# Both feed-forward down products with tokens stationary: 16 of 22 k tiles in two seven-product sets, sums added from PSUM, the first product's result turned back by transposes

## The chip, the cores and the metric

The kernel runs on one core of a Trainium2 chip. The metric is the device time of one launch in microseconds. Of the kernel before there are three timed runs and one profiled run.

## What is computed

One block of a language model, in float32, for 512 tokens of width 1024: a feed-forward part with half weight, a mixer (a gated convolution and gated linear attention, merged by sigmoid gates), a second feed-forward part with half weight, and a last norm.

```python
def swiglu(x, w_gu, w_down):
    g, u = jnp.split(x @ w_gu, 2, axis=-1)
    return (jax.nn.silu(g) * u) @ w_down          # w_gu 1024 x 5632, w_down 2816 x 1024

merged = jax.nn.sigmoid(ga) * y_conv + jax.nn.sigmoid(gb) * y_gla

for l in range(DEPTH):                            # DEPTH = 1
    x = x + 0.5 * swiglu(rmsnorm(x, norm_ffn1_g[l]), ffn1_w_gu[l], ffn1_w_down[l])
    x = x + hybrid_mixer(rmsnorm(x, norm_mix_g[l]), w_in[l], ...)
    x = x + 0.5 * swiglu(rmsnorm(x, norm_ffn2_g[l]), ffn2_w_gu[l], ffn2_w_down[l])
return rmsnorm(x, final_norm_g)
```

The change concerns the two products with `w_down` (22 tiles of 128 along k, 1024 outputs), what lies between the first one and the mixer, and the places at which the mixer loads the gates `gb`.

## The kernel before, in words

**Precision.** Every operand is split into a high part (a cast) and a low part (the rest), and every product is three matmuls: high x high, high x low, low x high. For weights the cast is made by ACT (L310) and the subtraction by DVE (L311); for activations the same pair stands at L550 and L551, in a norm at L416 and L417.

**Layout.** `x` is kept transposed, as eight tiles X of 128 features x 512 tokens. In most products the weights are stationary and 512 or 256 columns of tokens move. At the end X must have tokens in rows; so during the second feed-forward part's up product its blocks are turned by four PE transposes each (`natural`, L713), and the second down product has the tokens stationary and 512 columns of weights moving.

**Sets.** Where a matrix is taken as 2 x 2 blocks, a *set* computes its four block products as seven products (named m1, p2, q6, p5, q7, p4, p3) of sums and differences of blocks. That needs sums of weights (one by DVE, L297, and the rest by DMAs that accumulate, issued on POOL, L288), sums of activations (DVE, L530 to L537) and additions of the results, which share three pairs of PSUM banks: a (p2), b (m1, q6, q7, p4), c (p5, p3). A *wide set* is the form for the second down product: 8 k tiles, 512 tokens, 1024 outputs. Two of them take k tiles 0 to 15; each product has two units of four moving blocks, a step of the plan each. The last six k tiles are done plainly.

**Order of the work.** The weights' order is a hand-made list: `STEPS` has an entry for each unit that is cast, `PLAN` for each block that is loaded (L92 to L150). `W.take()` casts two steps ahead of use. The loads of a set are issued six steps ahead of its first product. Plain units are prefetched `early` steps ahead (L271 to L277; 5 in the feed-forward parts, 4 in the mixer), but the look ahead stops at the first step that belongs to a set. The order of the instructions on each engine is then made by the framework's scheduler from the order of the program and its waits.

**The first down product** (L682 to L705) is plain: weights stationary, 22 k tiles x 8 output tiles, eight PSUM banks. For each output tile in turn the last two k tiles are done, DVE adds half of the bank into X (L703), and `nxt.add` (L404 to L426) makes the norm's parts for the mixer: high part by ACT, low part by DVE, square by ACT, and its sum by DVE.

**The second down product** (`last_down`, L716 on) runs the wide sets in the order `SEQ` (L127): m1, p2, q6, p5, q7, p4, p3. ACT copies m1, q6 and q7 out of PSUM, scaled (L756); DVE adds a bank to such a copy (L759, L764, L773); POOL adds the sum to X (L761, L766, L775); p4 is added by DVE from PSUM into X (L769).

**The mixer** begins with q, k and the low-rank gate (`gate_k`, L934), which take the normed tiles in turn. POOL's queue saves all eight X tiles to DRAM (`xs`, L873). The gates ga and gb are computed, saved to DRAM (L1263 for gb) and read back by `gate` (a load on SP's queue at L1307 or L1309, a sigmoid on ACT, L1311). The eight tiles of gb are read within the two sets of `w_out_gla`, at their products m1, p5 and p4 (`gla_done`, L1340 on). The squares of the attention's output are cast at L389 and summed by PE at L1104.

## Time and profile before

| | |
|---|---|
| three timed runs, us | 1211.93, 1209.31, 1205.89; median 1209.31 |
| profiled run, us | 1207.32, its span 1205.6 |
| granted clock of TensorE, mean | 0.996 |
| first down product, first to last matmul | 231.18 to 350.89 us of the span |
| second down product's two wide sets | 1079.75 to 1165.93 us |
| POOL's instructions | 155, of them 108 accumulating DMAs |

How to read it: PE is TensorE's matmuls, PEld its weight loads, which overlap them; DVE is VectorE, ACT ScalarE, POOL GpSimd, SP the engine on whose queue the loads are issued. A row of the timeline has start, duration, engine, line, operation, output<-inputs and shape; in brackets stands how long the engine was idle ahead of it and what ended that. A row of a group has the count, then the total of busy time in us and the mean of one in ns, then the idle time ahead. A row of waits has the total in us, the number and the longest. A row of windows has the busy time of each engine, the granted clock, the share of DMA and GB/s.

### The profile page before, as it was taken

Reading aid. Unit: us, or ns where it says so; the run is one execution under the profiler, and the core shown is the slowest. Engines: PE = TensorE matmul, PEld = TensorE weight load, DVE = VectorE, ACT = ScalarE, POOL = GpSimd, SP = SyncE. Lnnn points to the kernel's source line nnn. Section 1 sums busy time; section 2 is a strip of 40 time slices with the busy share of each in tenths; the row PEclk is TensorE's granted clock in tenths of the full one; section 3 lists DMA queues with packets and bytes.
Section 4 is the critical chain, followed back from the end, with each engine's and each line's share of the span. In section 5 each row is a group of like instructions: output and inputs, shape, how many; then the busy total and the mean of one; then the engine's idle time right before and its main releaser. Section 6 shows DMA issues by size and latency. Waiting matters only on the chain.

```text
span 1205.6 us, 19145 instructions
## 1 busy us (share of the span) xinstructions
PE 1187.8 (99%) x7834; PEld 1092.1 (91%) x7834; DVE 840.7 (70%) x990; ACT 612.1 (51%) x762; POOL 130.0 (11%) x155
## 2 busy tenths in 40 slices
PE   9999999999999999999999999999999999999987
PEld 8899999988888889999999998898889999997776
DVE  7976666732277765868688687586597656589865
ACT  6555455532254465646554575454355455466453
POOL 0011111000010001101011100200001111113420
PEclk9999999999999999999999999999999999999999
DMA  9477777531162325767777756752447777757711
GB/s 349 95 200 189 178 187 186 167 105 53 52 241 92 88 70 150 213 171 186 194 184 176 192 182 183 208 149 93 161 99 194 189 175 177 183 143 197 161 50 70
DMA packets 59496, 190.81 MB, mean 158 GB/s; under 512 B 6576, under 2 KB 12848, under 8 KB 59408
## 3 DMA queue, kind: packets, MB, share of 16 engines
q1 hardware_dynamic: 37936, 124.27, 29.6%
q0 software_dynamic: 16832, 60.83, 27.3%
q10 hardware_dynamic: 4640, 4.49, 1.2%
q8 instruction: 61, 1.00, 0.3%
q14 instruction: 27, 0.22, 0.1%
HBM read 124.55 MB, written 8.39 MB: 110 GB/s over the span
## 4 chain that ended last, share of the span: by engine, by line
PE 89%; DVE 4%; DMA 3%; issue 2%; ACT 1%; POOL 0%; SPq 0%; DVEq 0%; ACTq 0%; POOLq 0%
PE mm L502 50%; PE mm L362 7%; PE mm L340 6%; PE mm L338 6%; PE mm L339 6%; DVE wl L311 2%; DMA f<-f 1%; PE mm L380 1%; PE mm L381 1%; PE mm L379 1%; DMA g<-gb 1%; DMA f<-wts 1%; PE aux L340 1%; PE aux L338 1%; PE aux L339 1%
## 5 line engine op out<-in xcount | busy, mean ns | idle before, releaser
L502 PE MATMUL mm<-op,wh 128*128 128x256 f32 x3584 | 649.9, 284 | 3.3 <-ACT tp L507 3.3
L310 ACT CAST wh<-f 128x1024 fp32r<-128x1024 f32 (+1 forms) x325 | 339.6, 1046 | 483.6 <-PE mm L502 225.2
L311 DVE TENSOR_TENSOR wl<-f,wh 128x1024 fp32r<-128x1024 f32 (+1 forms) x325 | 400.4, 1235 | 242.0 <-ACT wh L310 230.2
L502 PEld LDWEIGHTS mm<-op,wh 128*128 128x128 f32 x3584 | 560.2, 192 | 4.9 <-ACT tp L507 3.9
L502 PE MATMUL mm<-op,wl 128*128 128x256 f32 x1792 | 507.9, 284 | 0.0
L502 PEld LDWEIGHTS mm<-op,wl 128*128 128x128 f32 x1792 | 344.0, 192 | 0.1
L288 POOL DMA_DIRECT2D f<-f x108 | 93.3, 869 | 847.0 <-DVE wl L311 470.1
L340 PE MATMUL mm<-op,wl 128*128 128x512 f32 x324 | 126.4, 390 | 0.1
L338 PE MATMUL mm<-op,wh 128*128 128x512 f32 x324 | 126.5, 390 | 0.0
L339 PE MATMUL mm<-op,wh 128*128 128x512 f32 x324 | 126.1, 389 | 0.0
L340 PEld LDWEIGHTS mm<-op,wl 128*128 128x128 f32 x324 | 60.8, 188 | 13.2 <-DVE wl L311 0.5
L339 PEld LDWEIGHTS mm<-op,wh 128*128 128x128 f32 x324 | 60.8, 188 | 12.6
L338 PEld LDWEIGHTS mm<-op,wh 128*128 128x128 f32 x324 | 60.8, 188 | 12.4
L362 PE MATMUL mm<-op,wh 128*128 128x512 f32 x256 | 63.5, 390 | 0.3 <-DVE op L413 0.3
L362 PEld LDWEIGHTS mm<-op,wh 128*128 128x128 f32 x256 | 47.9, 188 | 10.6 <-ACT acc L422 0.4
L507 ACT COPY tp<-mm 128x512 f32<-128x512 f32 x96 | 55.8, 581 | 1.2 <-DVE tp L1238 1.0
L747 PE MATMUL mm<-wh,op 128*128 128x512 f32 x112 | 44.4, 398 | 4.1 <-ACT wh L310 2.4
L749 PE MATMUL mm<-wl,op 128*128 128x512 f32 x112 | 45.0, 401 | 2.1 <-DVE wl L311 2.0
L297 DVE TENSOR_TENSOR f<-f,f 128x1024 f32<-128x1024 f32 x36 | 44.0, 1221 | 1.8 <-DMA f<-f 1.0
L751 PE MATMUL mm<-wh,op 128*128 128x512 f32 x112 | 44.2, 395 | 0.0
L551 DVE TENSOR_TENSOR op<-hidw,op 128x1024 fp32r<-128x1024 f32 x28 | 36.0, 1297 | 1.3 <-ACT op L550 1.3
L550 ACT CAST op<-hidw 128x1024 fp32r<-128x1024 f32 x28 | 29.1, 1047 | 11.0 <-DVE hidw L597 4.0
(270 smaller groups left out, 1157.6 us busy)
## 6 DMA issues: line engine op xcount, KB each, us to landing
f<-wts SPq DMA_DIRECT2D x219, 512.0 KB, 4.3
f<-f POOLq DMA_DIRECT2D x108, 512.0 KB, 5.0
X<-xT SPq DMA_DIRECT2D x8, 256.0 KB, 4.9
xs<-X POOLq DMA_DIRECT2D x8, 256.0 KB, 5.4
ga<-tp ACTq DMA_DIRECT2D x8, 256.0 KB, 3.9
gb<-tp ACTq DMA_DIRECT2D x8, 256.0 KB, 4.1
g<-gb SPq DMA_DIRECT2D x8, 256.0 KB, 3.8
tp<-ga SPq DMA_DIRECT2D x8, 256.0 KB, 4.8
```

The source lines that it names most:

```text
L288: nc.gpsimd.dma_start(out_, a, accum_op=ALU.add)
L310: nc.scalar.copy(h[:, :w], raw[:, :w])
L311: nc.vector.tensor_tensor(out=l[:, :w], in0=raw[:, :w], in1=h[:, :w].bitcast(F32), op=ALU.subtract)
L338: nc.tensor.matmul(o, wh, ah, start=first, stop=False)
L339: nc.tensor.matmul(o, wh, al, start=False, stop=False)
L340: nc.tensor.matmul(o, wl, ah, start=False, stop=last)
L362: nc.tensor.matmul(o[c], w[:, s : s + P], a[k], start=k == 0 and j == 0, stop=k == kt - 1 and j == 2)
L502: nc.tensor.matmul(to, ww[:, s], aa[:, t], start=fresh and k == 0 and e == 0 and j == 0, stop=k == 3 and j == 2, skip_group_check=True)
L507: nc.scalar.copy(v, o)
L747: nc.tensor.matmul(o[t], bh[:, s], wh, start=fresh and k == 0, stop=False, skip_group_check=True)
L749: nc.tensor.matmul(o[t], bh[:, s], wl, start=False, stop=False, skip_group_check=True)
L751: nc.tensor.matmul(o[t], bl[:, s], wh, start=False, stop=k == 3, skip_group_check=True)
```

## The change

Four things are done.

1. The first down product takes the second one's form, and both are now one function, `down_product`: k tiles 0 to 15 as two wide sets, tokens stationary, then six plain k tiles. In the first, the results are kept in eight tiles `S_` (four token blocks x two halves of the outputs): the first result that comes to a tile is copied there by ACT, the others are added by DVE. The last four k tiles are done half by half; after each block of the second half, `back(i)` turns one 128-feature tile of the sum back by four transposes, DVE adds half of it into X, and `nxt.add(i)` follows. That does tiles 0 to 3; tiles 4 to 7 are done in `gate_k` of the mixer's k steps 0 to 3 (`norm.late`), and their save to DRAM with them.
2. The additions change in both. The order of the products is m1, p5, q6, p2, q7, p3, p4; no bank of the pair b is used by two products that follow each other. Pair a is kept over both sets and the plain k tiles: m1 of the first set is copied into it by ACT, and both sets' p2 and the plain tiles accumulate on it (the plain ones also on c, where the second set's p3 stays). Everything else DVE adds from PSUM, in the second product directly into X. POOL's twelve additions are gone. A class `DownOperands` makes the sums of activations, one of them already during the up product.
3. `Weights.fetch` looks past steps of sets, as long as the step being issued is one of a set. Two of the first product's last four weight units are put in the pool `op`, as the second product's are.
4. The eight tiles of gb are read and passed through the sigmoid during the eight steps of `w_out_conv` (`early_gate`), ahead of the sets of `w_out_gla`, into tiles that are free then.

```diff
-SEQ = ("m1", "p2", "q6", "p5", "q7", "p4", "p3")
+SEQ = ("m1", "p5", "q6", "p2", "q7", "p3", "p4")
...
-    if not slow:
-        wide_sets(down)
-    units(full(down, KF)[0 if slow else 8 * WIDE :])
+    wide_sets(down)
+    units(full(down, KF)[8 * WIDE :])
...
                 if p is None and n not in self.raw:
                     self.raw[n] = self.dma(n)
-                elif p is not None:
+                elif p is not None and STEPS[at][1] is None:
                     break
...
-            late = at >= len(STEPS) - TAIL
+            late = at >= len(STEPS) - TAIL or ENDS[0] - TAIL <= at < ENDS[0] - 2
...
+        def add(c, l, t, bank, scale):
+            at = 2 * l + t, c
+            if nxt is not None and at not in S_:
+                S_[at] = T()
+                nc.scalar.activation(S_[at], bank, AF.Copy, scale=2 * scale)
+                return
+            if nxt is not None:
+                nc.vector.scalar_tensor_tensor(out=S_[at], in0=bank, scalar=2 * scale,
+                                               in1=S_[at], op0=ALU.mult, op1=ALU.add)
+                return
+            x_ = block(c, l)[:, t]
+            nc.vector.scalar_tensor_tensor(out=x_, in0=grid(bank), scalar=scale, in1=x_,
+                                           op0=ALU.mult, op1=ALU.add)
+
+        A = [MM(), MM()]
...
+            banks = {"a": A, "b": [(MM, AUX)[w % 2]() for _ in range(2)], "c": [MM(), MM()]}
...
+                    if p == "m1" and w == 0:
+                        nc.scalar.copy(A[t], o[t])
+                    elif p == "m1":
+                        add(0, 0, t, o[t], 0.5)
+                    elif p == "q6":
+                        add(0, 1, t, o[t], 0.5)
+                    elif p in ("p5", "q7"):
+                        add(1, 1, t, o[t], -0.5)
+                    elif p == "p4":
+                        add(1, 0, t, o[t], -0.5)
+                    elif p == "p3" and w < WIDE - 1:
+                        add(0, 1, t, o[t], 0.5)
+            return banks["c"]
...
-        o = [[MM(), MM()] for t in range(NTB - 1)] + [[AUX(), AUX()]]
+        o = [[A[0], MM()], [A[1], MM()], [C[0], AUX()], [C[1], AUX()]]
...
+            def back(i):
+                o_ = MM()
+                for t in range(NTB):
+                    nc.tensor.transpose(o_[:, t * P : (t + 1) * P],
+                                        S_[t, i // 4][:, i % 4 * P : (i % 4 + 1) * P], ident)
+                nc.vector.scalar_tensor_tensor(out=x[i], in0=o_, scalar=0.5, in1=x[i],
+                                               op0=ALU.mult, op1=ALU.add)
+                nxt.add(i)
+
+            for e in range(2):
+                for t in range(NTB):
+                    for i in range(TAIL):
+                        mm(t, e, KF - TAIL + i, w[i], hl[i // 2])
+                    if e == 1 and t % 2 == 0:
+                        turned = halves(F32)
+                    to = turned[t % 2] if e else S_[t, e]
+                    nc.vector.tensor_tensor(out=to, in0=o[t][e], in1=S_[t, e], op=ALU.add)
+                    S_[t, e] = to
+                    if e == 1:
+                        back(t)
+            nxt.late = [lambda i=i: back(i) for i in range(NTB, KD)]
+            return
...
         def gate_k(k):
+            if k < NTB:
+                norm.late[k]()
+                nc.gpsimd.dma_start(xs[NTB + k], x[NTB + k])
...
+        def early_gate(i, a, l, t):
+            gb[i, a, l] = gate("gb", 4 * i + 2 * a, l, t)
...
+            if d < 4:
+                early_gate(0, d % 2, d // 2, vt[1][d])
+            else:
+                early_gate(1, d % 2, (d - 4) // 2, (E, M, KS, EX)[d - 4])
```

Three places show how the engines' orders change. In these rows the lines are those of the kernel whose order is shown; those of after lie one lower at the helpers (the weights' low part is L311 before and L310 after).

The first is DVE at the end of the first down product. Before (X the output tiles, op the norm's low parts, acc its sum of squares, wl the low part of a weight unit):

```order
L703 SCALAR_TENSOR_TENSOR X<-mm_2605,X 128x512
L417 SCALAR_TENSOR_TENSOR op_3256<-X,vec,op_3255 128x512
L426 TENSOR_TENSOR acc_3254<-acc_3254,tp_3269 128x512
L417 SCALAR_TENSOR_TENSOR op_3280<-X,vec,op_3279 128x512
L426 TENSOR_TENSOR acc_3254<-acc_3254,tp_3283 128x512
L703 SCALAR_TENSOR_TENSOR X<-mm_2606,X 128x512
L703 SCALAR_TENSOR_TENSOR X<-mm_2607,X 128x512
```

And after (L856 adds a bank of the second half to its tile of the sum, L845 adds a turned tile into X):

```order
L856 TENSOR_TENSOR op_3351<-mm_3208,tp_2920 128x512
L845 SCALAR_TENSOR_TENSOR X<-mm_3378,X 128x512
L416 SCALAR_TENSOR_TENSOR op_3361<-X,vec,op_3360 128x512
L425 TENSOR_TENSOR acc_3359<-acc_3359,tp_3386 128x512
L856 TENSOR_TENSOR op_3401<-aux_3209,tp_2702 128x512
L845 SCALAR_TENSOR_TENSOR X<-mm_3403,X 128x512
L416 SCALAR_TENSOR_TENSOR op_3410<-X,vec,op_3409 128x512
L425 TENSOR_TENSOR acc_3359<-acc_3359,tp_3413 128x512
L856 TENSOR_TENSOR op_3401<-aux_3210,tp_2704 128x512
L845 SCALAR_TENSOR_TENSOR X<-mm_3429,X 128x512
L310 TENSOR_TENSOR wl_3536<-f_3467,wh_3535 128x1024
```

The norm's instructions, which ran by themselves between the additions into X, now have one more addition per tile among them, and the mixer's first low parts of weights come between.

The second is DVE from the first to the second wide set of the second down product (wl the low parts of weights, L532, L537 and L551 sums and low parts of activations, hidw the activations). Before:

```order
L532 SCALAR_TENSOR_TENSOR hidw_8664<-hidw_8664 128x4x256
L311 TENSOR_TENSOR wl_11001<-f_10556,wh_11000 128x1024
L537 SCALAR_TENSOR_TENSOR hidw_8664<-hidw_8664 128x4x256
L764 SCALAR_TENSOR_TENSOR tp_11016<-mm_10925,tp_11016 128x512
L764 SCALAR_TENSOR_TENSOR tp_11020<-mm_10926,tp_11020 128x512
L311 TENSOR_TENSOR wl_11031<-f_10514,wh_11030 128x1024
L551 TENSOR_TENSOR op_11157<-hidw_8664,op_11156 128x1024
L297 TENSOR_TENSOR f_10935<-f_10927,f_10931 128x1024
L311 TENSOR_TENSOR wl_11047<-f_10552,wh_11046 128x1024
L769 SCALAR_TENSOR_TENSOR X_7776<-mm_10796,X_7776 128x4x128
```

And after (L571 and L589 are the sums and low parts of activations, L764 the additions from PSUM into X):

```order
L571 SCALAR_TENSOR_TENSOR hidw_8802<-hidw_8802 128x4x256
L589 TENSOR_TENSOR op_11275<-hidw_8802,op_11274 128x1024
L310 TENSOR_TENSOR wl_11133<-f_10692,wh_11132 128x1024
L764 SCALAR_TENSOR_TENSOR X_7920<-mm_10930,X_7920 128x4x128
L764 SCALAR_TENSOR_TENSOR X_7920<-mm_10931,X_7920 128x4x128
L310 TENSOR_TENSOR wl_11158<-f_10658,wh_11157 128x1024
L589 TENSOR_TENSOR op_11313<-hidw_8802,op_11312 128x1024
L296 TENSOR_TENSOR f_11068<-f_11060,f_11064 128x1024
L310 TENSOR_TENSOR wl_11174<-f_10696,wh_11173 128x1024
L764 SCALAR_TENSOR_TENSOR X_7920<-mm_10932,X_7920 128x4x128
```

The additions that went to tiles tp, for POOL to pass on, now go into X itself, and the kinds of work stand in much the same mixture.

The third is ACT in the mixer, at the squares of the fourth part of the attention's output (wh the high part of a weight unit, O and g the output and its squares, L389 before and L388 after the cast that PE needs for the sum of squares). Before:

```order
L1095 ACTIVATE O<-aux_5750,vec 128x512
L1097 ACTIVATE g_499_3625<-aux_5750 128x512
L310 CAST wh_5794<-f_5381 128x1024
L310 CAST wh_5834<-f_5385 128x1024
L1263 DMA gb<-tp_5822 128x2x256
L389 CAST tp_5825<-g_497_3623 128x512
```

And after (L1372 is the sigmoid of `gate`, with its table load):

```order
L1156 ACTIVATE O<-aux_5888,vec 128x512
L1158 ACTIVATE g_563_3763<-aux_5888 128x512
L1372 ACT_TABLE_LOAD
L1372 ACTIVATE g_564_3764<-g_564_3764 128x512
L309 CAST wh_5932<-f_5519 128x1024
L1372 ACTIVATE v_3486<-v_3486 128x512
L1372 ACTIVATE v_3487<-v_3487 128x512
L1372 ACTIVATE v_3488<-v_3488 128x512
L1372 ACTIVATE v_3489<-v_3489 128x512
L388 CAST tp_5963<-g_561_3761 128x512
```

Five of the eight gates, which stood in the sets of `w_out_gla`, now stand ahead of that cast.

More of the change, by code (lines that the diff above doesn't have):

```diff
@@ L665, in done @@
                         natural(i)
+                    for w in range(WIDE):
+                        if i == 4 * w + 4 - plain // 2:
+                            downs.append(down_operands(w))
+                            downs[w].early()
             return Set(xo, done)
@@ L680, in split_hid @@
             return h, l
[L682 to L705 removed]
+        down_product(full(down, KF), split_hid, downs, nxt)
     def natural(i):
@@ L732, in run_wide @@
                     ops.make(q)
-                b = {"m1": "b", "p2": "a", "q6": "b", "p5": "c", "q7": "b", "p4": "b",
+                n = {"m1": "b", "p2": "a", "q6": "b", "p5": "c", "q7": "b", "p4": "b",
                      "p3": "c"}[p]
-                fresh = b not in bank
-                if fresh:
-                    bank[b] = [MM(), MM()]
-                o = bank[b]
+                fresh = n not in used
+                used.add(n)
+                o = banks[n]
                 bh, bl = ops.get(p)
@@ L777, in last_down @@
+            return banks["c"]
         for w in range(WIDE):
-            run_wide(w)
+            C = run_wide(w)
         gr = []
-        for e in range(2):
+        for e in range(0 if nxt else 2):
             g = acc_row.tile([P, S], F32, tag=("acc", "row")[e], name=f"gr{e}")
@@ L871, in mixer @@
         gates_d = {n: dram.tile([KD, P, S], F32, tag=n, name=n) for n in ("ga", "gb")}
-        for k in range(KD):
+        for k in range(NTB):
             nc.gpsimd.dma_start(xs[k], x[k])
@@ L1340, in gla_done @@
         def gla_done(i):
-            sg = {}
             def done(s, p):
```

103 lines of the change are left out of this document (45 added, 58 removed).

## The prediction

> **What bounds the kernel now.** I read the page first, then the chain that ended last, then the stretches of the two down products by windows, then the waits in the second one, and last the engine that those waits name. The page:
>
> ```profile
> span 1205.6 us, 19145 instructions
> PE 1187.8 (99%) x7834; PEld 1092.1 (91%) x7834; DVE 840.7 (70%) x990; ACT 612.1 (51%) x762; POOL 130.0 (11%) x155
> PE 89%; DVE 4%; DMA 3%; issue 2%; ACT 1%; POOL 0%; SPq 0%; DVEq 0%; ACTq 0%; POOLq 0%
> ```
>
> PE is busy for 99% of the span and carries 89% of the chain, so a matmul taken out of a stretch that runs without gaps is worth its full spacing, and everything else matters only where PE waits. The profiled run took 1207.3 us (span 1205.6 and 1.7 around it). The three runs have a median of 1209.3 us, 2.0 above it, and go from 1205.9 to 1211.9. The sum below is made against 1207.3.
>
> The windows: first the second FFN's two wide sets whole, their first half, their second half, and then the first FFN's plain down product.
>
> ```profile
> core 0: us, PE busy (x) PEld busy (x) DVE busy (x) ACT busy (x) POOL busy (x), PEclk, DMA share, GB/s
> 1079.70:1166.00 86.30, 80.16 (x339) 63.66 (x339) 79.81 (x70) 52.50 (x59) 29.98 (x21) 0.98 0.61 153
> 1079.70:1122.00 42.30, 39.54 (x172) 31.38 (x171) 42.27 (x39) 27.49 (x31) 12.16 (x11) 1.00 0.70 174
> 1122.00:1166.00 44.00, 40.62 (x168) 32.28 (x169) 37.53 (x32) 25.01 (x29) 17.81 (x11) 0.96 0.52 132
> 231.00:351.00 120.00, 120.00 (x532) 99.40 (x532) 42.52 (x44) 33.74 (x38) 4.11 (x9) 1.00 0.31 107
> ```
>
> Two opposite stages. The plain product has PE busy in all of its 120.0 us, and DVE in 42.5. In the wide sets DVE is busy 42.27 of 42.30 us in the first set: it is level with PE or behind it. The change sends the first FFN's product from the first kind of stage to the second.
>
> **The matmuls.** First and last matmul of the plain product, one group of four transposes with the matmul behind it, and first and last step of the wide stretch:
>
> ```profile
> 231.18 0.40 PE L338 MATMUL aux<-op,wh 128*128 128x512 f32 x1
> 350.89 0.39 PE L362 MATMUL mm<-op,wh 128*128 128x512 f32 x1
> 920.16 0.60 PE L713 MATMUL aux<-ident,X 128*128 128x128 f32 x4
> 920.52 0.48 PE L502 MATMUL mm<-op,wh 128*128 128x256 f32 x2
> 1079.75 0.40 PE L747 MATMUL mm<-wh,op 128*128 128x512 f32 x1
> 1165.93 0.39 PE L790 MATMUL mm<-wh,op 128*128 128x512 f32 x1
> ```
>
> The plain product is 22 x 8 x 3 = 528 matmuls of 512 columns: (350.89 - 231.18) / 528 = 0.2267 us each, 119.7 us in all. In the new form each set has 7 products x 2 units x 2 k tiles x 2 token halves x 3 = 168, so two sets are 336; the remaining 6 k tiles x 4 token blocks x 2 halves x 3 are 144. That is 480, or 48 fewer: -10.9 us. The sum comes out with tokens in rows, so eight blocks are turned back by four transposes each: 920.52 - 920.16 = 0.36 us a block, +2.9. Net -8.0, with one answer as long as PE doesn't wait. In the second FFN the count of matmuls stays.
>
> **What the second FFN's wide sets lose now.** 336 matmuls at 0.2267 are 76.2 us; they took 1165.93 - 1079.75 = 86.2. So 10.0 us are lost. PE's own list of waits in the run, and the two large places:
>
> ```profile
> PE mm L749 <- DVE wl L311: 2.0, 4, 0.9
> 1108.09 0.39 PE L751 MATMUL mm<-wh,op 128*128 128x512 f32 x1
> 1110.19 0.50 PE L747 MATMUL mm<-wh,op 128*128 128x512 f32 x1 [1.72 <-ACT tp L756]
> 1146.59 0.39 PE L751 MATMUL mm<-wh,op 128*128 128x512 f32 x1
> 1149.33 0.50 PE L747 MATMUL mm<-wh,op 128*128 128x512 f32 x1 [2.35 <-ACT wh L310]
> 1150.77 0.50 PE L749 MATMUL mm<-wl,op 128*128 128x512 f32 x1 [0.95 <-DVE wl L311]
> 1152.11 0.63 PE L751 MATMUL mm<-wh,op 128*128 128x512 f32 x1
> 1152.54 0.63 PE L747 MATMUL mm<-wh,op 128*128 128x512 f32 x1
> 1141.27 5.99 DMA f<-wts
> ```
>
> (1) 1108.09 to 1110.19 is 2.10, 1.9 over a spacing: p4 continues q7's bank and waits until ACT has copied it out. The new order puts p3, which has another bank, behind q7, and no two neighbours share bank b: gone. (2) 1146.59 to 1149.33 to 1150.77 is 4.18 for two spacings (0.45), so 3.7 lost; then matmuls stand 1152.54 - 1152.11 = 0.43 apart, nine of them, 9 x 0.20 = 1.8 more. The cause is the last row: the load of the unit behind the sets began only at 1141.27 and took 5.99, since the prefetch stops while a set step is being issued. The new condition lets it look past, so the unit is loaded up to five steps earlier, some 5 x 12 x 0.2267 = 13.6 us: gone, with its slow matmuls. (3) The other 10.0 - 1.9 - 5.5 = 2.6 are waits for the low parts of weights, which DVE makes late (three of the four waits in the first row). These depend on DVE.
>
> The slow matmuls have a rule in the Trainium skill, "TensorE: Matmul & The Clock Gate", Part 1: the clock falls to half after one idle window of about 3.4 us and needs as long to rise. Here 0.43 against 0.2267 does look like half a clock, but the gap of PE before it was 2.5 us and then 1.2, shorter than that window, and the recovery came within 4 us. By the rule's number these gaps would cost 3.7 and not 5.5; I take the measured 5.5.
>
> **DVE, the engine that decides.** The durations: the first row and the third from the wide stretch, the second from 60:215 where POOL adds nothing, the others from the whole run or the wide stretch.
>
> ```profile
> L311 DVE TENSOR_TENSOR wl<-f,wh 128x1024 fp32r<-128x1024 f32 x29 | 40.7, 1420 | 0.0
> L311 DVE TENSOR_TENSOR wl<-f,wh 128x1024 fp32r<-128x1024 f32 x54 | 65.9, 1223 | 41.7 <-ACT wh L310 41.7
> L551 DVE TENSOR_TENSOR op<-hidw,op 128x1024 fp32r<-128x1024 f32 x11 | 15.4, 1414 | 0.0
> L764 DVE SCALAR_TENSOR_TENSOR tp<-mm,tp 128x512 f32<-128x512 f32 x4 | 2.6, 677 | 0.0
> L537 DVE SCALAR_TENSOR_TENSOR hidw<-hidw 128x1024 f32<-128x1024 f32 x4 | 4.9, 1213 | 0.0
> L761 POOL TENSOR_TENSOR X<-X,tp 128x512 f32<-128x512 f32 x4 | 7.1, 1781 | 3.0 <-DVE tp L759 3.0
> L766 POOL TENSOR_TENSOR X<-X,tp 128x512 f32<-128x512 f32 x4 | 8.1, 2053 | 31.6 <-DVE tp L764 31.6
> L775 POOL TENSOR_TENSOR X<-X,tp 128x512 f32<-128x512 f32 x4 | 9.8, 2467 | 6.4 <-DVE tp L773 6.4
> ```
>
> The same subtraction takes 1.42 us beside POOL's twelve adds (25.0 us) and 1.22 without. The change drops these adds and lets DVE add from PSUM straight into X, so I take 1.22. The Trainium skill, "SBUF — State Buffer", § Who interferes with whom, says that a DVE operation with two SBUF inputs and a GpSimd operation that reads SBUF exclude each other for the whole instruction. By it DVE could get back up to POOL's 25 us; the rows show 40 long operations at +0.2, some 8 us, and I go by these.
>
> A new set costs DVE 14 low parts of weights and 7 of operands at 1.22, 2 sums of weights and 3 of operands at 1.21, and adds at 0.68: ten in either set of the second FFN, four and eight in the first's, where ACT's copies start the sums. That is 25.6 + 6.1 + 6.8 = 38.5, against PE's 168 x 0.2267 = 38.1; in the first FFN 34.4 and 37.1. DVE is just level: no long stall, but a product whose low parts queue behind adds and sums may wait. I put 1 us on each set of the first FFN (0 to 2.5, the upper end from half of today's 10.0 per set) and 1 on each of the second (0.5 to 2.5). So the first FFN's sets cost +2 (0 to 5) and the second FFN's go from 10.0 to 2, that is -8 (-9 to -5). What hides the transposes' and the norm's DVE work is the tail's matmuls, next.
>
> **The handover to the mixer.** Before, each output tile was added and normed while the next one's matmuls ran. Now the last four k tiles run half by half; behind each block of the second half one tile is turned back, added and normed, and four more tiles follow between the mixer's first k steps.
>
> ```profile
> L416 ACT ACTIVATE op<-X,vec 128x512 fp32r<-128x512 f32 x23 | 16.4, 713 | 7.3 <-DVE X L703 3.8 <-DVE X L1383 3.0 <-DMA X<-xT 0.4
> L417 DVE SCALAR_TENSOR_TENSOR op<-X,vec,op 128x512 fp32r<-128x512 f32 x24 | 17.9, 746 | 1.1 <-ACT op L416 0.8
> L426 DVE TENSOR_TENSOR acc<-acc,tp 128x512 f32<-128x512 f32 x21 | 14.4, 683 | 0.0
> ```
>
> A step of four k tiles is 12 x 0.2267 + 0.36 = 3.1 us of PE. DVE has two adds (0.68 each), a low part (0.75) and a sum of squares (0.68): 2.8 us, covered, but the last tiles share DVE with the mixer's weights. +0.5 (0 to 3). Without cover, each of the four late tiles would show its chain, 0.36 + 0.68 + 0.71 + 0.75 = 2.5 us, which is a rival. xs is saved later for the upper four tiles, on POOL's queue; it is read again only after the mixer: nothing.
>
> **The mixer's gates.** ACT's rows now, and PE's waits for ACT:
>
> ```profile
> PE mm L502 <- ACT tp L507: 3.3, 3, 1.8
> 710.55 1.28 ACT L1311 ACT_TABLE_LOAD   x1 [2.45 <-DMA g<-gb]
> 779.96 0.63 ACT L1311 ACTIVATE g<-g 128x512 f32<-128x512 f32 x1 [4.53 <-DMA g<-gb]
> 603.14 0.62 ACT L389 CAST tp<-g 128x512 fp32r<-128x512 f32 x1 [0.21 <-issue]
> 604.20 0.40 PE L1104 MATMUL aux<-tp,ones_r 128*128 128x512 f32 x1
> ```
>
> At 779.96 a gate blocks ACT until its load has landed, and PE waits 1.8 behind the copy that follows; loaded early, this goes: -1.8. The first gate of the next stage stands in the new order where it stood (its table load at 710.55 is another of the three waits): stays. But five of the early gates, with a table load, are put ahead of the cast at 603.14, which PE needs 1.1 us later: 1.28 + 5 x 0.63 = 4.4 us of ACT, partly idle there. I take +1.8, between 0 and 4.4. Sum 0 (-1.8 to +2.6).
>
> **The sum.** 1207.3 - 10.9 + 2.9 + 2 + 0.5 - 8 + 0 = 1193.8. With half of the 2.0 us by which the median lies above the profiled run, 1195.
>
> **The rivals.**
> (a) No new wait at all: DVE keeps ahead in all four sets and the early gates find ACT idle: 1207.3 - 8.0 - 9 - 1.8 = 1188.5. For it: 1.22 is a duration, and DVE's work of 34.4 to 38.5 is under or at PE's. Against: DVE had no reserve in the first window. 0.18.
> (b) The handover shows its chain at each of the late tiles: 4 x 2.5 = 10 in place of 0.5: 1204. For it: each late k step needs the tile turned just ahead. Against: weights of the four gates give 12 matmuls a step or more to hide behind. 0.08.
> (c) The low parts stay at 1.42 though POOL adds nothing (the adds from PSUM or the transfers being what slows them): DVE's set is 38.5 + 21 x 0.2 = 42.7, 4.6 over PE's, in four sets 18.4 in place of the 4 us booked: 1208, no change. For it: 174 GB/s of transfers are in that window too. 0.07.
> (d) The other side: the same lateness, and each wait of a microsecond or two brings the slow matmuls, as at 1152.11. With two such trips a set, 2 x 1.8 + 4.6 = 8.2 a set, 33 in four: 1207.3 - 8.0 - 10.0 + 33 = 1222. It decides from about 6.5 us a set on. Against: the short waits of the first set, under 0.6 each, left its clock at 1.00. 0.04.
> (e) The prefetch doesn't get past the sets, for want of free buffers: the 5.5 stay: 1200. For it: the two halves of a set hold all ten buffers. Against: its last products free them one by one. 0.08.
>
> **How the numbers follow.** My own case has 0.55, its own range is 1189 to 1200. With (a) below and (e), (b) above, the range is 1186 to 1205, and leaves out (c), (d) and the edges. A measurement of this kernel tells 0.5% from no change, 6.0 us on 1209.3: faster is under 1203.3. Faster: 0.55 + 0.18 + 0.08 and half of (b), 0.85. Same: (c) and the other half of (b), 0.11. Slower: (d), 0.04.
>
> **What would show it.** Right: PE without gaps at p4's start and at the unit behind the sets; low parts at about 1.22 in the wide sets; a first down product of some 110 to 114 us up to the last of its own matmuls; clock 1.00 in all four sets; at the squares of the fourth gate output a new wait of about 2 us. Wrong: low parts at 1.4, DVE without idle time in the first FFN's sets, PE waiting for wl in every product, or waits for op at the mixer's first steps.

## The result and the profile after

| | before | after |
|---|---|---|
| median, us | 1208.78 (4 runs, 1205.89 to 1211.93) | 1197.47 (4 runs, 1195.71 to 1198.95) |
| ratio of the times | | 0.9909, 95% interval 0.9888 to 0.9929 |
| span of the profiled run, us | 1205.6 | 1194.6 |

The change made the kernel 11.3 us faster; the forecast was 1195 with a range of 1186 to 1205. The page of after, its first rows:

```profile
span 1194.6 us, 19198 instructions
PE 1179.0 (99%) x7818; PEld 1086.8 (91%) x7818; DVE 878.7 (74%) x1044; ACT 630.3 (53%) x780; POOL 116.3 (10%) x155
```

PE has 16 instructions fewer (48 matmuls less, 32 transposes more), DVE 54 more, and POOL as many as before: its twelve additions went, and twelve accumulating transfers for the first product's sets came.

Where the time went is read from four landmarks of PE's timeline: the first matmul of the first down product, a step of the mixer that is the same in both kernels (the first one behind the transposes of the gates), the first matmul of the second down product, and its first plain k tile. PE runs as many instructions between the second and the third of them in both kernels (4601). Of before, only the second landmark has not been shown:

```profile
456.58 0.36 PE L502 MATMUL mm<-op,wh 128*128 128x256 f32 x1
```

Of after, with the first plain k tile of the first product (308.70) as well:

```profile
231.84 0.40 PE L789 MATMUL mm<-wh,op 128*128 128x512 f32 x1
308.70 0.39 PE L823 MATMUL mm<-wh,op 128*128 128x512 f32 x1
451.03 0.36 PE L501 MATMUL mm<-op,wh 128*128 128x256 f32 x1
1077.77 0.40 PE L789 MATMUL mm<-wh,op 128*128 128x512 f32 x1
1154.96 0.39 PE L823 MATMUL mm<-wh,op 128*128 128x512 f32 x1
```

| stage | before, us | after, us | difference | forecast |
|---|---|---|---|---|
| up to the first down product | 231.18 | 231.84 | +0.7 | 0 |
| first down product to the mixer's landmark | 225.40 | 219.19 | -6.2 | -8.0 + 2 + 0.5 = -5.5 |
| from there to the second down product | 623.17 | 626.74 | +3.6 | 0 (-1.8 to +2.6) |
| its two wide sets | 86.18 | 77.19 | -9.0 | -8 |
| the rest (span less the last landmark) | 39.67 | 39.64 | 0 | 0 |

The sum is -11.0, the difference of the spans. Two stages came out a little better than forecast, the mixer worse than its range. The +0.7 ahead of the first down product lies in a stage that the change leaves alone, with 1726 instructions of PE in both.

The sets, by windows: the first product's two, the second's two, and the first of these.

```profile
231.80:310.00 78.20, 77.84 (x344) 64.13 (x343) 67.79 (x67) 50.95 (x56) 10.04 (x13) 1.00 0.74 191
1077.70:1154.90 77.20, 76.52 (x338) 62.96 (x338) 72.00 (x74) 47.26 (x48) 8.53 (x10) 1.00 0.67 169
1077.70:1116.00 38.30, 38.30 (x171) 31.73 (x171) 38.15 (x39) 25.01 (x26) 5.23 (x7) 1.00 0.77 194
```

336 matmuls at 0.2267 us are 76.2. The first product's sets took 308.70 - 231.84 = 76.9 and lose 0.7, the second's took 77.2 and lose 1.0, where before lost 10.0. The clock is 1.00 in all three rows. In the second product's first set DVE is still busy 38.15 of 38.30 us, as it was before, and yet PE waits for nothing there; an experiment below takes that up. DVE's low parts of weights in the second product's sets, now 1.217 us where before had 1.420:

```profile
L310 DVE TENSOR_TENSOR wl<-f,wh 128x1024 fp32r<-128x1024 f32 x29 | 35.1, 1217 | 1.6 <-ACT wh L309 1.6
```

PE's list of waits in the run is now led by two in the mixer:

```profile
PE aux L1165 <- ACT tp L388: 4.3, 1, 4.3
PE mm L501 <- ACT tp L506: 1.5, 1, 1.5
```

The first is the squares of the fourth attention output, behind the sigmoids that were put ahead of their cast. ACT's timeline, and PE's:

```profile
595.96 0.63 ACT L1372 ACTIVATE v<-v 128x512 f32<-128x512 f32 x1 [1.19 <-DMA v<-gb]
597.87 0.63 ACT L1372 ACTIVATE v<-v 128x512 f32<-128x512 f32 x1 [1.28 <-DMA v<-gb]
600.01 1.30 ACT L1372 ACTIVATE v<-v 128x512 f32<-128x512 f32 x2 [1.51 <-DMA v<-gb]
601.22 0.60 ACT L388 CAST tp<-g 128x512 fp32r<-128x512 f32 x1
601.87 0.79 PE L1165 MATMUL aux<-tp,ones_r 128*128 128x512 f32 x1 [4.26 <-ACT tp L388]
```

Three times ACT waits for the load of a sigmoid's tile, 4.0 us in the three brackets, and the cast stands behind all of them. The second place is near 798 us, in the sets of `w_out_gla`. POOL's and ACT's rows there:

```profile
767.39 4.31 POOL L1438 DMA_DIRECT2D X<-xs  x8 [6.09 <-DVE op L550]
774.62 0.89 POOL L287 DMA_DIRECT2D f<-f  x1 [2.92 <-DVE wl L310]
782.51 1.05 ACT L309 CAST wh<-f 128x1024 fp32r<-128x1024 f32 x1 [3.21 <-DMA f<-f]
792.99 0.88 POOL L287 DMA_DIRECT2D f<-f  x1 [17.48 <-DVE wl L310]
797.88 1.04 ACT L309 CAST wh<-f 128x1024 fp32r<-128x1024 f32 x1 [4.29 <-DMA f<-f]
```

X is brought back from DRAM by eight loads; the accumulating transfer issued at 774.62, just behind them, lands for the cast at 782.51, 7.9 us later, where the next one takes 4.9 (792.99 to 797.88). The casts behind it run late from there on, and the next transfer is too late for PE.

### The profile page after: what moved, and what is told of

Read it like the earlier page. It is cut to its first block, busy times and chain, and to the rows that moved or that the text cites. A ratio compares the mean times of both kernels' runs of the same rounds, so it can differ in the third digit from the quotient of the medians.

```text
span 1194.6 us, 19198 instructions
## 1 busy us (share of the span) xinstructions
PE 1179.0 (99%) x7818; PEld 1086.8 (91%) x7818; DVE 878.7 (74%) x1044; ACT 630.3 (53%) x780; POOL 116.3 (10%) x155
## 5 line engine op out<-in xcount | busy, mean ns | idle before, releaser
L309 ACT CAST wh<-f 128x1024 fp32r<-128x1024 f32 (+1 forms) x335 | 350.2, 1047 | 436.7 <-PE mm L501 226.0
L501 PEld LDWEIGHTS mm<-op,wh 128*128 128x128 f32 x3584 | 560.4, 192 | 2.6 <-ACT tp L506 1.7
L310 DVE TENSOR_TENSOR wl<-f,wh 128x1024 fp32r<-128x1024 f32 (+1 forms) x335 | 406.9, 1217 | 179.9 <-ACT wh L309 174.9
L501 PEld LDWEIGHTS mm<-op,wl 128*128 128x128 f32 x1792 | 344.1, 192 | 0.6 <-DVE wl L310 0.4
L287 POOL DMA_DIRECT2D f<-f x120 | 103.5, 865 | 927.0 <-DVE wl L310 506.1
L339 PE MATMUL mm<-op,wl 128*128 128x512 f32 x192 | 75.0, 391 | 0.5 <-DVE wl L310 0.5
L337 PE MATMUL mm<-op,wh 128*128 128x512 f32 x192 | 75.2, 392 | 0.2 <-ACT wh L309 0.2
L338 PE MATMUL mm<-op,wh 128*128 128x512 f32 x192 | 74.7, 389 | 0.0
L361 PE MATMUL mm<-op,wh 128*128 128x512 f32 x256 | 64.0, 392 | 0.0
L791 PE MATMUL mm<-wl,op 128*128 128x512 f32 x160 | 62.4, 390 | 0.7 <-DVE wl L310 0.7
L789 PE MATMUL mm<-wh,op 128*128 128x512 f32 x160 | 62.3, 389 | 0.0
L793 PE MATMUL mm<-wh,op 128*128 128x512 f32 x160 | 62.3, 389 | 0.0
L361 PEld LDWEIGHTS mm<-op,wh 128*128 128x128 f32 x256 | 48.0, 189 | 10.2
L339 PEld LDWEIGHTS mm<-op,wl 128*128 128x128 f32 x192 | 36.0, 188 | 8.4 <-DVE wl L310 1.0
L337 PEld LDWEIGHTS mm<-op,wh 128*128 128x128 f32 x192 | 36.0, 188 | 7.7 <-ACT wh L309 0.4
L338 PEld LDWEIGHTS mm<-op,wh 128*128 128x128 f32 x192 | 36.1, 188 | 7.4
L791 PEld LDWEIGHTS mm<-wl,op 128*128 128x128 f32 x160 | 30.1, 188 | 7.4 <-DVE wl L310 1.3
L793 PEld LDWEIGHTS mm<-wh,op 128*128 128x128 f32 x160 | 30.0, 188 | 6.2
```

Of the source, the lines that this page charges most:

```text
L287: nc.gpsimd.dma_start(out_, a, accum_op=ALU.add)
L309: nc.scalar.copy(h[:, :w], raw[:, :w])
L310: nc.vector.tensor_tensor(out=l[:, :w], in0=raw[:, :w], in1=h[:, :w].bitcast(F32), op=ALU.subtract)
L337: nc.tensor.matmul(o, wh, ah, start=first, stop=False)
L338: nc.tensor.matmul(o, wh, al, start=False, stop=False)
L339: nc.tensor.matmul(o, wl, ah, start=False, stop=last)
```

## The experiments

The theory after reading both profiles: the first product's gain is the count of matmuls; the second's is that DVE is on time; the mixer loses at the squares. The rivals are in the expectations: that the prefetch made the second product's gain (the forecast's own step), that DVE has no time left, that the low parts were slow from transfers and not from POOL. All are medians over several runs, and ratios are against the kernel before on the same chip. After's 1197.47 is from a session of its own; before's median lay between 1208.13 and 1209.18 in these sessions, so a difference of a microsecond to after says nothing.

**The first product alone.** It is plain again (`slow` marks the first feed-forward part), with `nxt.add` after each output tile, and the rest is as after.

```diff
-    wide_sets(down)
-    units(full(down, KF)[8 * WIDE :])
+    if not slow:
+        wide_sets(down)
+    units(full(down, KF)[0 if slow else 8 * WIDE :])
...
+        for d in range(KD):
+            for i in range(2):
+                mm(d, KF - 2 + i, w[i], hl)
+            nc.vector.scalar_tensor_tensor(out=x[d], in0=o[d], scalar=0.5, in1=x[d],
+                                           op0=ALU.mult, op1=ALU.add)
+            nxt.add(d)
```

> The first down product plain again (weights stationary, 528 matmuls, no transposes, all eight tiles normed in turn), everything else as after the change. Theory: the first product's gain is 48 matmuls less 32 transposes, less what its wide sets and the handover lose, 6.2 us from the first matmul of the product to the mixer's first later landmark. So +6 us on 1197.5, about 1203.5, and the second product's sets stay at 77.2 us. Rival: the plain form hands over to the mixer sooner than the trace lets see, and the change in the first product was worth under 3 us: at most 1200.5.

1203.02 us (1202.44 to 1203.79), 5.6 more than after. The theory holds: half of the change's gain is the first product's shorter count, less what its sets and the handover lose. In the profiled run the stage up to the mixer's landmark took 225.4 again (232.06 to 457.43), 6.2 more than after. The second product's sets took 78.4 (1083.67 to 1162.06), where 77.2 was expected.

**The prefetch, taken out of the change, and put alone into the kernel before.**

```diff
-                elif p is not None and STEPS[at][1] is None:
+                elif p is not None:
                     break
```

> The prefetch stops at set steps again, everything else as after. Theory: behind the second product's sets the cast of a unit that has not landed stands in ACT's queue ahead of a set's cast again, about 5.5 us lost there, and the same can come behind the first product's sets: 1203, up to 1208 if both. Rival: the new order of the products and the shorter DVE work already cover it: within 1.5 us of 1197.5. The wait of PE near 798 us (1.6 us, for an accumulating transfer) tells apart whether the earlier loads slow that transfer (then it goes) or whether it was merely uncovered when the gates went (then it stays).

1197.32 us: nothing. The second product's sets ran from the first of these rows to the second:

```profile
1078.56 0.40 PE L789 MATMUL mm<-wh,op 128*128 128x512 f32 x1
1156.19 0.39 PE L823 MATMUL mm<-wh,op 128*128 128x512 f32 x1
```

77.6 us, 0.4 more than after. PE's wait near 798 us stayed too, so it was not the earlier loads that made it. The other way round, the edit reversed on the kernel before:

> The kernel before with nothing but the new prefetch rule. The forecast's step: the wait at the unit behind the second product's sets is there because the prefetch stops at set steps, so 5.5 us go, about 1203. Theory now, after the run with the old rule in the changed kernel lost nothing: the load waited for a buffer that DVE's late low parts freed late, and looking ahead doesn't free it: 1207 to 1209, the wait of PE behind a cast near 1149 us stays.

1208.81 us, ratio 0.9996 (0.9978 to 1.0013). The sets took 84.9 us, and the waits are there:

```profile
PE mm L747 <- ACT tp L756: 2.9, 2, 1.7
PE mm L747 <- ACT wh L310: 1.3, 1, 1.3
```

So the prefetch rule is worth nothing measurable by itself, and taking it out costs nothing: the forecast's step on it is wrong. The chain of waits of before has the answer, of which the forecast shows only the last row:

```profile
1138.60 2.32 DVE wl L311
1140.91 0.24 SPq L284
1141.27 5.99 DMA f<-wts
```

The load that came late followed the end of a low part on DVE: it waited for a buffer that DVE still read. Looking further ahead frees no buffer.

**POOL's additions.** In the kernel before, they are made by DVE from the same tiles, and nothing else is changed.

```diff
-                        nc.gpsimd.tensor_tensor(out=x_, in0=x_, in1=grid(y), op=ALU.add)
+                        nc.vector.tensor_tensor(out=x_, in0=x_, in1=grid(y), op=ALU.add)
```

(in three places, one of them with `subtract`)

> The kernel before, with POOL's twelve additions into X made by DVE from the same tiles, nothing else. Theory: without POOL's reads the low parts take 1.22 us, which gives back more than the twelve additions (0.68 each, 8.2) cost; DVE is on time and the wait at the unit behind the sets goes with the waits for low parts: the sets lose 2 to 4 us in place of 10.0, the bank wait of 1.9 among them: 1201 to 1203. Rival: the additions eat what the contention gives back; the sets lose 8 or more.

1202.87 us, ratio 0.9952 (0.993 to 0.9974). DVE's low parts in the sets, the sets' first matmul, and the first plain k tile:

```profile
L311 DVE TENSOR_TENSOR wl<-f,wh 128x1024 fp32r<-128x1024 f32 x30 | 36.4, 1221 | 0.5 <-ACT wh L310 0.5
1084.13 0.40 PE L747 MATMUL mm<-wh,op 128*128 128x512 f32 x1
1161.12 0.39 PE L790 MATMUL mm<-wh,op 128*128 128x512 f32 x1
```

The sets took 77.0 us and lose 0.8 in place of 10.0, more than expected: the bank wait of 1.9 went too, though p4 still follows q7 on the same bank. Before, ACT's copy of that bank stood behind a cast that waited for DVE:

```profile
1108.60 1.05 ACT L550 CAST op<-hidw 128x1024 fp32r<-128x1024 f32 x1 [1.75 <-DVE hidw L532]
1109.55 1.08 ACT L756 ACTIVATE tp<-mm 128x512 f32<-128x512 f32 x2
```

All three losses that the forecast booked apart (the bank, the late unit, the late low parts) were one: DVE was late, because POOL was adding. The sets gained 9.2 and the time 6.3 only: in the profiled run the sets began at 1084.13 in place of 1079.75, behind a wait of PE for a gate's load that was 5.0 us here and 1.8 in before's profile, in a place that the edit leaves alone. The converse, twelve additions on POOL put beside the changed kernel's second product (they write a spare tile and are of no use):

```diff
+                    if nxt is None and p in ("q6", "q7", "p4"):
+                        x_ = block(*{"q6": (0, 1), "q7": (1, 1), "p4": (1, 0)}[p])[:, t]
+                        nc.gpsimd.tensor_tensor(out=grid(T()), in0=x_, in1=x_, op=ALU.add)
```

> The change, and beside it twelve additions on POOL in the second product's sets that read X and write a spare tile, so many as before the change. Theory: beside them DVE's low parts take 1.4 us again, DVE falls behind, buffers of loads come free later, and the wait at the units behind the sets comes back: the two sets go from 77.2 to 80 to 85 us, 1200 to 1205. Rival: the 1.42 us of before came from the transfers; then low parts stay at 1.22 and the sets within 1 us of 77.2.

1202.27 us (1200.31 to 1205.09), 4.8 more than after. In the second product's sets, low parts by DVE and POOL's additions:

```profile
L310 DVE TENSOR_TENSOR wl<-f,wh 128x1024 fp32r<-128x1024 f32 x29 | 40.5, 1405 | 0.1
L810 POOL TENSOR_TENSOR tp<-X 128x512 f32<-128x512 f32 x10 | 15.0, 1585 | 22.6 <-DVE X L764 22.6
```

and the sets' first matmul and the first plain k tile:

```profile
1076.67 0.40 PE L789 MATMUL mm<-wh,op 128*128 128x512 f32 x1
1159.22 0.39 PE L826 MATMUL mm<-wh,op 128*128 128x512 f32 x1
```

82.6 us, 6.4 lost. The low parts are at 1.4 again, with no more transfers than in after (158 GB/s, after 169): POOL's additions make them slow, and PE waits for them. There is a rival: the additions stand on the queue that issues the accumulating transfers, and could hold these up. Here they didn't: ahead of each of its ten issues in the sets POOL was idle, 33.5 us in all, and waited for DVE. In the kernel before two issues did go out right behind an addition (1133.28, behind 6.26 us of POOL), and what that adds to its 10.0 was not separated.

**More work for DVE.** One 512-wide operation per product in all four sets, with a result that nothing uses.

```diff
+EXTRA = ("m1", "p5", "q6", "p2", "q7", "p3", "p4")
...
+                if p in EXTRA:
+                    spare = T()
+                    for _ in range(1):
+                        nc.vector.tensor_tensor(out=spare, in0=bh[:, :S].bitcast(F32),
+                                                in1=bl[:, :S].bitcast(F32), op=ALU.add)
```

> One more 512-wide DVE operation per product in all four wide sets, 7 x 0.68 = 4.8 us a set, about the lateness that the forecast's third rival priced at 4.6 a set. Theory now: only the second FFN's first set has no DVE time left (38.15 busy of 38.30), the other three have 4 to 5 us idle each, so it costs 4 to 6 us in all: 1202 to 1204. Rival, the forecast's own pricing: it costs its full length in all four, 18 us: 1215.

1197.12 us: nothing, and neither expectation holds. The first product's sets and the second's, by windows:

```profile
231.30:307.80 76.50, 76.50 (x339) 63.29 (x339) 73.92 (x78) 50.07 (x56) 11.40 (x13) 1.00 0.75 194
1076.30:1152.50 76.20, 76.20 (x338) 63.14 (x338) 75.78 (x84) 45.05 (x46) 8.55 (x10) 1.00 0.68 171
```

DVE is busy 75.78 of 76.20 us, and PE waits for nothing at all; with the new operations the scheduler's order is another one, and even the 1.0 us of waits is gone. DVE's busy time in the second product's sets rose by 3.8 us only for 9.6 of new operations, since four low parts for the plain k tiles, which after makes within the sets, came behind them. A DVE that is busy all the time is not yet a DVE that is late. Part of it is how durations count: the last section shows low parts that follow each other at less than their duration.

**The banks.** p4 and p3 change places in the changed kernel, so that p4 follows q7 on the same pair of banks, in all four sets.

```diff
-SEQ = ("m1", "p5", "q6", "p2", "q7", "p3", "p4")
+SEQ = ("m1", "p5", "q6", "p2", "q7", "p4", "p3")
```

> The changed kernel with p4 ahead of p3, so that p4 follows q7 on the same pair of banks; in all four sets. Theory: at each p4 PE waits until DVE has added q7's bank, about the 1.9 us of before or somewhat less, since two banks are used in turn: 4 x 1 to 1.9 = 4 to 7.6, so 1201.5 to 1205. Rival: DVE adds the first bank while PE still fills the second, and the wait is under 0.5 us each: 1199.5 or less.

1211.15 us (1209.99 to 1216.77), 0.3% slower than the kernel before: ratio 1.0032 (1.0013 to 1.005). Four waits at the sets' banks:

```profile
PE aux L789 <- DVE tp L760: 3.4, 1, 3.4
PE aux L789 <- DVE X L764: 3.3, 1, 3.3
PE mm L789 <- DVE tp L760: 2.1, 1, 2.1
PE mm L789 <- DVE X L764: 1.6, 1, 1.6
```

10.4 us in the four rows, more than expected: the addition that empties the bank stands in DVE's queue behind whatever low parts are there. The other 3 us of the 13.7 over after are not all accounted for; behind the longest wait matmuls stood 0.43 us apart in place of 0.2267 (from 307.52 on). Since DVE empties the banks itself, the new order of the products is a condition of the whole change, which without it would lose its gain.

**The gates.** They are read in the sets of `w_out_gla` again, the rest as after.

```diff
...
+                if p == "m1":
+                    sg[0, 0] = gate("gb", 4 * i, 0, E)
+                if p == "p5":
+                    sg[1, 1] = gate("gb", 4 * i + 2, 1, M)
+                    sg[1, 0] = gate("gb", 4 * i + 2, 0, KS)
+                if p == "p4":
+                    sg[0, 1] = gate("gb", 4 * i, 1, EX)
...
```

> The gates gb are read within the w_out_gla sets again, everything else as after. Theory: the wait of 4.4 us at the squares of the fourth output, with the slow matmuls behind it some 5.5, is made by the sigmoids ahead of the cast and goes; the two waits of before (1.3 and 2.0) come back: 1195 to 1196, faster than the whole change by about 2. Rival: the squares wait for something else, now that PE arrives 5.5 us sooner; then the wait stays and the gates' waits are added: 1200 or more.

1195.28 us (1195.16 to 1197.51), by the medians 2.2 faster than the whole change; their ranges overlap (after's lowest is 1195.71), so the sign rests on the trace: the wait at the squares is gone from it, as the theory has it. What came back is another wait than expected: one of 4.4 us, behind a gate whose load took 10.4 us (ACT's row, and the load's in the chain):

```profile
777.02 0.63 ACT L1372 ACTIVATE g<-g 128x512 f32<-128x512 f32 x1 [7.07 <-DMA g<-gb]
766.51 10.43 DMA g<-gb
```

Then the gates early, but tied, so that they cannot go ahead of the squares:

```diff
         def early_gate(i, a, l, t):
+            nc.scalar.copy(t[:, 0:1], m[d][:, 0:1])
             gb[i, a, l] = gate("gb", 4 * i + 2 * a, l, t)
```

> The early gates stay in the w_out_conv steps, but each tile is first touched by a one-column copy of that step's result, so that its load and its sigmoid cannot move ahead of the squares. Theory: the squares' wait and its slow matmuls go (5.5) and no gate waits in the sets; the wait near 798 stays: 1191 to 1193. Rival: the loads of gb, tied to products, hold up the weights behind them on SP's queue, and PE waits in w_out_conv or in the sets instead: 1196 or more.

1197.37 us: no gain, the rival's time. The squares don't wait, but PE waits for ACT three times, 7.1 us, in the sets and ahead of them, the longest (3.7) for an accumulating transfer that took 13.1 us, by the chain:

```profile
PE mm L501 <- ACT tp L506: 7.1, 3, 3.7
770.77 13.10 DMA f<-f
```

The rival named the weights behind the gates on SP's queue; here the wait was for a transfer of POOL's queue, which is a third way.

**X brought back later.** In all of these, whatever transfer falls into the stretch of 767 to 783 us is slow; what is common to them is X's eight loads. So they are held back until the second set's p2, by a copy of one column into the tiles; first with the gates in the sets, then with the tied gates, then in the kernel before.

```diff
+            nc.vector.tensor_copy(XS[-1][:, :, 0:1], two(2)[:, 0, 0:KD].unsqueeze(2))
             for k in range(KD):
                 nc.gpsimd.dma_start(x[k], xs[k])
...
-hooks={(0, "p3"): [reload]}
+hooks={(1, "p2"): [reload]}
```

> Gates gb read in the sets as before, and the eight loads that bring X back from DRAM (2 MB, issued by POOL in the middle of the first w_out_gla set) held back until the second set's p2 is done, by a copy of one column. Theory: in those 20 us the transfers are the bound; the gate that PE waited 4.55 us for took 10.4 us to load because X was loaded at the same time, so the wait shrinks under 1 us: 1191. X is needed only some 25 us later. Rival: the weights' loads alone make it slow and the wait keeps over 2 us: 1193.5 or more; or X lands too late for the mixer's last additions and PE waits there.

1189.22 us (1188.99 to 1189.59), ratio to before 0.9843 (0.982 to 0.9866). ACT's first gate in the sets waits 0.78 us, X's loads go out at 799.23, and PE's longest wait for DVE is 0.6:

```profile
770.77 0.63 ACT L1372 ACTIVATE g<-g 128x512 f32<-128x512 f32 x1 [0.78 <-DMA g<-gb]
799.23 4.31 POOL L1439 DMA_DIRECT2D X<-xs  x8 [11.65 <-DVE X L1437]
PE mm L791 <- DVE wl L310: 0.6, 1, 0.6
```

> Early gates tied to the w_out_conv steps, and X brought back later as well. Theory: of the three waits left with the tied gates, the one of 3.9 us for an accumulating transfer that took 13.1 us and the one of 1.7 us behind it go, since they shared the transfer engines with X; the one of 2.05 at the end of w_out_conv stays: about 1191. Rival: tied gates crowd the weights' loads by themselves and at least half of the 5.6 us stays: 1194 or more.

1190.20 us (1188.72 to 1190.98): about the same. With X out of the way it makes no difference that can be seen whether the gates are early or in the sets.

> The kernel before, with nothing but X brought back from DRAM later (behind the second w_out_gla set's p2). Theory: the gate that PE waited 2.0 us for near 780 us took 7.9 us to load because X was loaded with it, so that wait goes: 2 to 3 us, about 1205.5. Rival: the gate's own late issue makes the wait; it stays at 1 us or more and the time within 1 us of 1208.3.

1202.52 us, ratio 0.9954 (0.994 to 0.9968): 6.7 less than before, more than the theory's 2 to 3. The gate that PE had waited for near 780 us waits 0.68 for its load:

```profile
775.54 0.63 ACT L1311 ACTIVATE g<-g 128x512 f32<-128x512 f32 x1 [0.68 <-DMA g<-gb]
```

In the two profiled runs the second product began at 1079.75 and at 1075.5, 4.2 us sooner. The wait at the gate makes 2.0 of that, counted from matmul to matmul, and the slow matmuls behind it some 1.6 more: from 782.92 to 786.13 before's granted clock was 0.50. The median gained more, 6.7. The wait differs from one profile to the next (5.2 us with the new prefetch alone and 5.0 with the additions on DVE, both with before's gates), and the runs of before spread from 1202.94 to 1211.14, those with X late from 1201.13 to 1203.87. That the wait is longer in before's slower runs would account for the rest, but their traces are not there to show it.

## Why the prediction was right, point by point

- **The count of matmuls** (-8.0, and 1 us of waits for each of the first product's sets): right, and confirmed by undoing it alone (5.6 by the medians). The sets lose 0.7 where 2 was booked, and the rest of the way to the landmark, the handover in it, 1.1 where 0.5 was: 6.2 gained for 5.5.
- **The second product's sets** (10.0 to 2): right in size (1.0 left), wrong in two of three causes. Step (1) put 1.9 on the bank, step (2) 5.5 on the prefetch, and only the last 2.6 on DVE. The prefetch alone gave 0.4 us in after's sets and nothing in either time, so rival (e) priced a loss that was not there; POOL's additions alone gave 9.2 of the 10.0. The forecast named POOL's effect on the low parts, with 1.22 against 1.42, and then looked for separate causes of the two large waits. The chain ahead of each, which shows DVE as the first link, was not followed back. Step (1)'s rule on the banks does hold, but as a thing that the new form needs: against it the same change came out at 1211.
- **DVE's time.** 38.5 and 34.4 us of work a set were added up from durations, and the forecast called DVE level with PE; its third rival priced 4.6 us of lateness a set, its fourth 8.2. The added 4.8 us a set cost nothing. That is a term sized by a wrong measure: the durations of operations that follow each other overlap, and busy time close to the span says little on lateness. The third rival's condition, low parts at 1.4, was made in two sets by POOL's additions put beside the change: these lost 6.4 us, where 4.6 a set makes 9.2. So its price was too high even there, and the mere length of DVE's list cost nothing.
- **The mixer** (0): wrong by 3.6. The place at the squares was named, with bounds of 0 and 4.4, and 1.8 taken: PE's wait was 4.3. The forecast counted the sigmoids' own time; the loads they waited for in turn, 4.0 us, made it long. Behind the wait matmuls were slow for a while, at a granted clock of 0.50 from 602.47 to 606.52, a cost that the forecast left out here: from the landmark to the start of `w_out_conv` (718.86 before, 718.85 after), after took 5.5 us more, although one gate's wait of 1.3, which the forecast had kept, was gone. And the gate near 780 went as forecast (-1.8), but what was late next was not asked: the accumulating transfer behind X's loads, 1.5 at 798.
- **The handover**: small, as forecast; the tail of the first product loses 0.4 us beyond its matmuls and transposes.

```profile
342.81 0.60 PE L843 MATMUL mm<-ident,tp 128*128 128x128 f32 x4
```

Ahead of the transposes at 342.81 lie its 144 matmuls, 32.6 us, and three such groups, 1.1, in 342.81 - 308.70 = 34.1 us.

The number came out because the errors were small against two terms: 8.0 counted on PE, which was understood, and some 9 in the second product's sets, which stood there to be taken whatever the cause. In the second there is luck: the steps on the bank and on the prefetch led to the right total for reasons that the runs don't bear out. The errors of the stages (+0.7, -0.7, +3.6, -1.0) also cancel in part.

## What to carry to other kernels

When several waits of one stretch have different names, follow the chain ahead of each back to its first link before giving each its own cause and its own repair: here three names were one engine that another engine slowed. Ask of work that is moved earlier what it will stand ahead of, and what its loads will share the transfers with; and ask of a wait that goes what lands next. A bulk load that is needed late (X, whose loads after issues from 767.39 on and which it first reads at 826.62) should be issued late: that edit gave 6.7 us to the kernel before and, with the gates put back, 8.3 to the changed one.

## What the runs showed of the hardware

- Long operations on DVE that follow each other start closer than they last. In the kernel before with its additions on DVE:

```profile
1108.84 1.22 DVE L311 TENSOR_TENSOR wl<-f,wh 128x1024 fp32r<-128x1024 f32 x1
1109.98 1.22 DVE L551 TENSOR_TENSOR op<-hidw,op 128x1024 fp32r<-128x1024 f32 x1
1111.11 1.22 DVE L311 TENSOR_TENSOR wl<-f,wh 128x1024 fp32r<-128x1024 f32 x1
```

1.13 to 1.14 from start to start, against a duration of 1.22. In such a row, sums of durations overstate DVE's work by some 7%.

- POOL's additions lengthen DVE's subtractions from 1.22 to 1.41 us on average. The average hides what happens: only the operations beside an addition are long, and those by much. In the run with additions put beside the change, POOL and DVE:

```profile
1095.38 2.36 POOL L810 TENSOR_TENSOR tp<-X 128x512 f32<-128x512 f32 x2
1095.64 3.19 DVE L310 TENSOR_TENSOR wl<-f,wh 128x1024 fp32r<-128x1024 f32 x1
```

This low part took 1.98 us more than its 1.21 beside two additions of 2.36 together: it ended 1.09 after POOL did. Where a DVE operation came between the two additions, the pair took 3.02 and the two DVE operations beside it, 1.68 and 2.06, were 1.3 longer than alone (1107.46 to 1111.56): POOL waited as well. The rule of the Trainium skill that the forecast weighed ("SBUF — State Buffer", § Who interferes with whom) is that one of the two blocks for the whole instruction. This trace agrees with it. By it the busy time of POOL (15.0 us in these sets) still overstates what DVE loses, since it holds POOL's own waits: DVE's subtractions of weights and activations were 7.1 us longer in all than in after, 5.5 of that in 29 low parts, 29 x (1.405 - 1.217).

- A wait of PE can cost more than its length. In before, a wait of 1.84 us (up to 782.06) was followed by 3.2 us at a granted clock of 0.50, and after's wait of 4.26 by 4.1 us; behind after's wait of 1.45 (up to 799.46) the clock stayed at 1.00. What decides between them is not shown.

- A transfer of 512 KB took 4.9 us with X's eight loads over, 7.9 right behind them, and 13.1 in the run with the tied gates; a gate of 256 KB took 10.4 beside them.
